# The last 1024 columns of an output projection by seven half-size products, with the weights' sums kept in DRAM

## The chip, the cores and the metric

The kernel runs on one core of a Trainium2 chip. The metric is the device time of one execution in microseconds (us), the median of several. The engines of the core are named as in the profile: PE (TensorE, the matmuls), DVE (VectorE), ACT (ScalarE), POOL (GpSimd) and SP (SyncE, which here only issues DMAs). ACT and POOL issue DMAs too. Matmul results go to PSUM banks of 128 partitions by 512 float32; everything else lies in SBUF or, for what is put aside, in DRAM.

## The reference

One layer of an encoder on 512 tokens with 2048 model columns, in float32. Eight stick-breaking heads and eight latent heads read the normed input; their gated outputs form `mixed`, 512 x 2048, and the last step is a projection, a norm and a residual:

```python
h = rms_norm(x, pre_norm_w)
p = h @ w_in                                    # all projections of the heads
o_a = stick_breaking_attention(q, k, v)         # 8 heads x 128
o_b = chunk_causal_softmax_attention(q_mla, k_mla, v_mla)   # 8 latent heads x 128
mixed = concat([o_a * silu(sb_gate), o_b * silu(mla_gate)], axis=-1)
y = mixed @ w_out                               # 512 x 2048 by 2048 x 2048
return x + rms_norm(y, post_norm_w)
```

## The kernel before

Each float32 operand of a product is held as a high and a low part (both float32r). `split` makes them: ACT casts the high part (line 96), DVE subtracts it from the value for the low part (line 99). A product of two such operands is three matmuls into the same bank, high by high, high by low and low by high (`mm3`, line 127).

TensorE runs its matmuls in the order in which they are traced. The loads on SP (`load`, line 88) keep their traced order too. A scheduler orders the rest: ACT, DVE and POOL each run their instructions one after another in an order that was fixed when the kernel was built, and each instruction waits there for its inputs and for its buffer.

The program has these stages. The latents `cq` and `ckv` are made first, to about 108 us. Then come the latent heads, to about 310 us. One iteration of their loop (line 685) is about 20 to 26 us; the filler between attention steps is the gate columns (`gps`). In an iteration POOL issues the loads of the next small weights (`mraw`, line 114), clears a part of the transposed rows `th` and `tl` (lines 588 and 589), and stores the gated head to DRAM (`put_aside`, line 607). Then come the stick-breaking heads, whose filler is the other projections and the first steps of the output projection.

The output projection `y = mixed @ w_out` has four groups of 512 columns. `out_group` makes groups 0 to 2. Each has eight weight pieces of 512 KB (two chunks of 128 rows each): SP loads a piece into the ring `raw` of N_RAW = 2 buffers, ACT casts `whi` from it, DVE subtracts `wlo`, and both of these have rings of three buffers. A chunk is multiplied with the four blocks of 128 tokens of `mixed`, whose parts (`mxh`, `mxl`, one pair for each chunk, in `msplit`) were loaded back from DRAM by POOL (line 392). One group is 16 chunks x 4 blocks x 3 = 192 matmuls of 512 columns. Group 0 ends at about 717 us, group 1 at about 760.5 and group 2 at about 804. During group 2 `resident_weights` splits ten of the last group's sixteen chunks (`woh`, `wol`).

The last group goes block by block, so that each block's norm and residual run beside the next block's products: 48 matmuls a block, and for the last block 2 x 48 of 256 columns. For each block SP loads four pieces of x (`xr`), PE makes the bank, ACT squares it (line 408) for the norm, DVE multiplies it by the norm's weight (line 410), POOL makes the factor `r` (lines 791 and 792), DVE makes the four residual pieces (line 801), and their DMAs go out alternately on SP and ACT (line 802). On SP's queue the `xr` loads of a block stand behind the two `out` DMAs of the block before it.

Of the kernel before, what the change touches and what calls it, by code (L numbers as in the profile page):

```python
# [19 lines left out]
P = 128  # L20
S = 512
# [36 lines left out]
def block(ctx: ExitStack, tc: tile.TileContext, a: dict):  # L58
# [61 lines left out]
    # TensorE runs what is traced, in that order: the order below keeps it fed.  # L120
# [131 lines left out]
    def turns(n, unit, name):  # L252
        """fraction of a turn in n * unit radians, n a whole number of at most 12 bits"""
# [34 lines left out]
    # [block, half, 32]: cosines twice; sines with the sign of their half; the queries' ones scaled  # L288
# [23 lines left out]
    def latent(banks, n, width, name):  # L312
        """The scaled projection, token-major, and the sums of squares of its first n columns."""
# [23 lines left out]
    done = {}  # L337

    def gate(t, name):
        """silu of a tile of gate columns, transposed."""  # L340
# [35 lines left out]
    # chunks of the output projection: the latent heads' first  # L376
# [24 lines left out]
    ypw = [[] for _ in range(NB)]  # L401
    y_tags = iter(["q4"] * 4 + ["row"] * 6 + ["gt"] * 2 + ["tr"] * 5)

    def out_piece(b, ps, pw):
        n = len(ypw[b])
        w = ps.shape[1]
        junk = zbank("junk")
        act.activation(out=junk[:, :w], in_=ps, func=AF.Square, scale=1.0 / math.sqrt(D), accum_out=ssy[b][:, n:n + 1])
        y = g(f"y{b}", tag=next(y_tags))[:, :w]
        dve.tensor_tensor(out=y, in0=ps, in1=pw, op=ALU.mult)  # L410
        ypw[b].append(y)

    def post_weight(gi):
        pw = g("pw", tag="tr")
        load(out=pw, in_=a["post_w"][0:1, gi * S:(gi + 1) * S].broadcast_to([P, S]))
        return pw

    w_tags = iter(["t"] * 4 + ["mv"] * 4 + ["g"] * 22)
    ws = []

    def resident_weights():
        """The next two chunks of the last columns' weights."""
        raw = ring.tile([P, 1024], F32, tag="raw", name="raw", bufs=N_RAW)
        load(out=raw, in_=a["w_o"][3, len(ws) // 2])
        for j in range(2):
            hi, lo = g("woh", F32R, next(w_tags)), g("wol", F32R, next(w_tags))
            split(hi, lo, raw[:, j * S:(j + 1) * S])
            ws.append((hi, lo))

    def out_group(gi):  # L430
        banks = [bank(f"y{b}") for b in range(NB)]
        for i in range(8):
# [4 lines left out]
            if gi == 2 and i >= 3:  # L437
                resident_weights()
            for j in range(2):
                s_ = slice(j * S, (j + 1) * S)  # L440
                split_mixed()
                for b in range(NB):
                    out_mm(banks[b], b, i * 2 + j, wh[:, s_], wl[:, s_])
                    yield
        pw = post_weight(gi)
        for b in range(NB):
            out_piece(b, banks[b], pw)

    def filler():
# [10 lines left out]
        for gi in range(3):  # L460
            yield from out_group(gi)

# [14 lines left out]
    def rotary_queries(grp, new_bank):  # L477
# [11 lines left out]
        # the two blocks of a bank are one accumulation, which the first of its products starts  # L489
# [24 lines left out]
    def rotary_turn(stacks):  # L514
        """[high; low] of four heads' rotary queries, transposed."""
# [27 lines left out]
    # rstd of every token along the free axis, on every partition  # L543
# [27 lines left out]
    def row_tiles(name):  # L571
        """The rows of the four blocks of queries, the short ones beside each other."""
# [3 lines left out]
    class Weighted:  # L576
        """(sum over s of vals[s, :]^T rows[q, s]) * gate, transposed, by blocks of keys."""
# [46 lines left out]
    class Latent:  # L624
        """Scores and softmax of a latent head."""
# [59 lines left out]
    for h in range(H + 1):  # L685
# [47 lines left out]
    for h in range(H):  # L733
# [4 lines left out]
        for b in range(NB):  # L738
# [11 lines left out]
            fill((1, 3, 3, 7)[b])  # L750
        cur = Weighted(rows, need("v", h // 4), (h % 4) * P)
# [7 lines left out]
        else:  # L759
            put_aside(h, out)  # L760

# [1 line left out]
    for _ in steps:  # L763
        pass
    pw = post_weight(3)
    for i in range(5, 8):
        wh, wl = weights(a["w_o"][3, i], 1024)
        ws += [(wh[:, :S], wl[:, :S]), (wh[:, S:], wl[:, S:])]
    for b in range(NB):
        xs = []  # L770
        for i in range(2):
            if b % 2:
                xr = [g("xr"), g("xr")]
            else:
                xr = ring.tile([P, 1024], F32, tag="raw", name="xr", bufs=N_RAW)
                xr = [xr[:, :S], xr[:, S:]]
            for j in range(2):
                load(out=xr[j], in_=a["x"][b * P:(b + 1) * P, (2 * i + j) * S:(2 * i + j + 1) * S])
            xs += xr
        cuts = [slice(0, S)] if b < NB - 1 else [slice(0, 256), slice(256, S)]  # L780
        part = tn("part")
        for n, s_ in enumerate(cuts):
            ps = bank(f"y{b}")[:, :s_.stop - s_.start]
            for c in range(16):
                out_mm(ps, b, c, ws[c][0][:, s_], ws[c][1][:, s_])
            if n == len(cuts) - 1:
                dve.tensor_reduce(out=part, in_=ssy[b][:, :3 + n], axis=AX.X, op=ALU.add)
                dve.tensor_scalar(out=part, in0=part, scalar1=EPS, scalar2=None, op0=ALU.add)
            out_piece(b, ps, pw[:, s_])
        r2 = tn("r2")  # L790
        pool.tensor_tensor(out=r2, in0=ssy[b][:, 2 + len(cuts):3 + len(cuts)], in1=part, op=ALU.add)
        pool.tensor_tensor(out=r2, in0=r2, in1=mhalf[:, :1], op=ALU.pow)
        at = 0
        for i, y in enumerate(ypw[b]):
            w = y.shape[1]
            o = xs[at // S][:, at % S:at % S + w]
            if b == NB - 1 and i == 2:
                act.activation(out=y, in_=y, func=AF.Copy, scale=r2)
                pool.tensor_tensor(out=o, in0=y, in1=o, op=ALU.add)
            else:  # L800
                dve.scalar_tensor_tensor(out=o, in0=y, scalar=r2, in1=o, op0=ALU.mult, op1=ALU.add)
            (nc.sync, nc.scalar)[i % 2].dma_start(out=a["out"][b * P:(b + 1) * P, at:at + w], in_=o)
            at += w
# [54 lines left out]
```

## Time and profile before

| what | value |
|---|---|
| time, median of 3 runs | 858.51 us (858.46 to 859.05) |
| span of the profiled execution | 857.2 us |
| PE busy | 844.1 us (98%), 4146 matmuls |
| DVE busy | 425.0 us (50%) |
| ACT busy | 337.8 us (39%) |
| POOL busy | 42.1 us (5%) |
| mean granted TensorE clock | 0.997 |
| DMA | 97.19 MB, mean 113 GB/s |

The span is the time from the first to the last instruction of one profiled execution; the median time is 1.3 us longer. A matmul's own duration in the trace overlaps that of the next, so the distance between the starts of two matmuls is what one of them costs. An engine's idle time is listed with what ended it, the releaser. The names of tiles are those of the code; "128x512 f32" is partitions by elements. Rows of DMA issues on SP and ACT (SPq, ACTq) show when the DMA was issued, not when it landed.

### The profile page before, as it was taken

How to read it: one execution, taken by the hardware profiler on the slowest of the kernel's cores; microseconds unless marked ns; L12 is line 12 of the kernel's file. 1: busy time of each engine (PE TensorE's matmuls, PEld its weight loads, DVE VectorE, ACT ScalarE, POOL GpSimd, SP SyncE). 2: the span in 40 equal slices, each digit the busy share in tenths (PEclk: the TensorE clock that was granted, in tenths of full speed). 3: DMA queues.
4: the chain of work that ended last, by engine and by line, in shares of the span. 5: the costliest groups of instructions: out<-in, count | busy, mean ns of one | idle time of the engine just before them, and what ended most of it. 6: DMA issues, size and time to landing. Idle time of an engine off the chain costs nothing.

```text
span 857.2 us, 10780 instructions
## 1 busy us (share of the span) xinstructions
PE 844.1 (98%) x4146; PEld 711.9 (83%) x4146; DVE 425.0 (50%) x757; ACT 337.8 (39%) x585; POOL 42.1 (5%) x100
## 2 busy tenths in 40 slices
PE   8999999999999999999999999999999999999995
PEld 5889988888888888888888888888888888888885
DVE  5576755556556433536354524446364623244333
ACT  6743655554454423424243314323243423134201
POOL 1010000000000110000000000000001000000001
PEclk9999999999999999999999999999999999999998
DMA  9823222222221252222222224222223232336364
GB/s 314 317 75 101 99 86 75 81 93 80 93 81 62 76 192 97 79 100 85 97 88 86 89 96 135 99 86 95 89 81 132 97 110 99 111 103 204 112 190 153
DMA packets 32627, 97.19 MB, mean 113 GB/s; under 512 B 4144, under 2 KB 4672, under 8 KB 32576
## 3 DMA queue, kind: packets, MB, share of 16 engines
q1 hardware_dynamic: 27792, 82.46, 28.5%
q0 software_dynamic: 3488, 12.08, 4.3%
q10 hardware_dynamic: 1296, 1.97, 0.7%
q8 instruction: 32, 0.52, 0.3%
q14 instruction: 19, 0.16, 0.1%
HBM read 88.37 MB, written 8.13 MB: 113 GB/s over the span
## 4 chain that ended last, share of the span: by engine, by line
PE 93%; DVE 3%; ACT 1%; DMA 1%; issue 0%; POOL 0%; DVEq 0%; SPq 0%; ACTq 0%; POOLq 0%
PE y L122 20%; PE gps L122 19%; PE qp L122 10%; PE v L122 10%; PE kp L122 10%; PE cq L122 4%; PE av L122 4%; PE mz L122 3%; PE mqp L122 3%; PE ckv L122 2%; PE tp L125 2%; PE z L122 2%; PE qrp L122 1%; PE mv L122 1%; PE mkp L122 1%; DMA raw<-in_w_cq 1%
## 5 line engine op out<-in xcount | busy, mean ns | idle before, releaser
L99 DVE TENSOR_TENSOR wlo<-raw,whi 128x1024 fp32r<-128x1024 f32 (+2 forms) x124 | 147.5, 1190 | 187.8 <-ACT whi L96 186.0
L96 ACT CAST whi<-raw 128x1024 fp32r<-128x1024 f32 (+2 forms) x124 | 127.0, 1024 | 251.5 <-PE y L122 58.4
L122 PE MATMUL gps<-hh,whi 128*128 128x512 f32 x256 | 102.0, 398 | 0.0
L122 PE MATMUL gps<-hl,whi 128*128 128x512 f32 x256 | 100.1, 391 | 0.0
L122 PE MATMUL gps<-hh,wlo 128*128 128x512 f32 x256 | 99.9, 390 | 0.0
L122 PE MATMUL y<-whi,mxh 128*128 128x512 f32 (+1 forms) x222 | 85.5, 385 | 0.0
L122 PE MATMUL y<-whi,mxl 128*128 128x512 f32 (+1 forms) x222 | 85.1, 383 | 0.0
L122 PE MATMUL y<-wlo,mxh 128*128 128x512 f32 (+1 forms) x222 | 85.1, 383 | 0.0
L122 PEld LDWEIGHTS gps<-hh,wlo 128*128 128x128 f32 x256 | 48.1, 188 | 10.6
L122 PEld LDWEIGHTS gps<-hl,whi 128*128 128x128 f32 x256 | 48.2, 188 | 7.6
L122 PEld LDWEIGHTS gps<-hh,whi 128*128 128x128 f32 x256 | 48.2, 188 | 7.5
L122 PE MATMUL qp<-hh,whi 128*128 128x512 f32 x128 | 52.0, 407 | 0.0
L96 ACT CAST th<-tp 128x512 fp32r<-128x512 f32 (+1 forms) x64 | 27.1, 423 | 63.2 <-PE tp L125 63.2
L99 DVE TENSOR_TENSOR tl<-tp,th 128x512 fp32r<-128x512 f32 (+1 forms) x64 | 31.2, 488 | 39.9 <-ACT th L96 39.5
L122 PE MATMUL v<-whi,hh 128*128 128x512 f32 x128 | 50.9, 397 | 0.0
L122 PE MATMUL qp<-hh,wlo 128*128 128x512 f32 x128 | 50.1, 391 | 0.0
L122 PE MATMUL qp<-hl,whi 128*128 128x512 f32 x128 | 50.0, 391 | 0.0
L122 PE MATMUL v<-whi,hl 128*128 128x512 f32 x128 | 49.9, 390 | 0.0
L122 PE MATMUL v<-wlo,hh 128*128 128x512 f32 x128 | 49.9, 390 | 0.0
L122 PE MATMUL kp<-hh,whi 128*128 128x512 f32 x128 | 49.8, 389 | 0.0
L122 PE MATMUL kp<-hl,whi 128*128 128x512 f32 x128 | 49.8, 389 | 0.0
L122 PE MATMUL kp<-hh,wlo 128*128 128x512 f32 x128 | 49.8, 389 | 0.0
(246 smaller groups left out, 1618.5 us busy)
## 6 DMA issues: line engine op xcount, KB each, us to landing
raw<-in_w_t SPq DMA_DIRECT2D x64, 512.0 KB, 3.2
raw<-in_w_o SPq DMA_DIRECT2D x32, 512.0 KB, 3.2
raw<-in_w_v SPq DMA_DIRECT2D x16, 512.0 KB, 3.2
xs<-in_x SPq DMA_DIRECT2D x16, 256.0 KB, 6.2
xr<-in_x SPq DMA_DIRECT2D x16, 256.0 KB, 4.9
xt<-in_xt SPq DMA_DIRECT2D x15, 256.0 KB, 5.7
mixed<-mix POOLq DMA_DIRECT2D x15, 256.0 KB, 2.3
mx<-mixed POOLq DMA_DIRECT2D x15, 256.0 KB, 3.4
```

The source lines that it names most:

```text
L96: i = act.copy(out=hi, in_=src)
L99: dve.tensor_tensor(out=lo, in0=src, in1=hi.bitcast(F32), op=ALU.subtract)
L122: tc.keep_in_program_order(pe.matmul(out=out, lhsT=lhsT, rhs=rhs, start=start, stop=stop, **kw))
L125: tc.keep_in_program_order(pe.transpose(out, in_, identity))
```

## The change

Groups 0 and 1 stay. Groups 2 and 3 are now one product of 512 tokens x 2048 by 2048 x 1024, cut in halves: tokens A1 and A2 of 256, K of 1024, columns of 512. The Strassen-Winograd scheme makes the four quarters of the result from seven products instead of eight. Each product is 8 chunks x 2 blocks x 3 = 48 matmuls of 512 columns (`product`), and the last one is made block by block, its second block in halves of 256 columns. The order is x = A11 w11, z = S1 (w_sums 0), y = S2 (w_sums 2), v = S3 (w_sums 1) and into the same banks A22 (w_sums 3), then A12 w21 into the banks of x, then S4 w22. S1 to S4 are sums of quarters of `mixed`; w_sums 0 to 3 are sums of quarters of the weights.

`weight_sums(j)` makes the weights' sums: four loads of 256 KB by POOL, four DVE subtractions 128x512, four stores of 256 KB to DRAM by POOL. It is called eight times, 32 of each in all (16.8 MB moved). They are traced among the stick-breaking heads; the order that is built puts them among the latent heads. `first_sums` and `last_sum` load chunks of `mixed` again and make and split S1, S2, S4 (groups 0 and 1) and S3, which takes the place of a part of `msplit`. The last head's chunk is now put in DRAM too. The ring `raw` has four buffers in place of two. The `xr` tiles come from other slots. The results of the block pair 2, 3 are complete first, so their residuals come first.

```diff
-SLOTS = {"g": 46, "q4": 4, "row": 6, "tr": 4, "t": 4, "gt": 2, "mv": 4, "qrt": 8}
-N_RAW = 2
+SLOTS = {"g": 48, "q4": 4, "row": 6, "tr": 4, "t": 4, "gt": 2, "mv": 4, "qrt": 8}
+N_RAW = 4
...
+    def sum_piece(b, at, ps, u, pw, junk):
+        w = ps.shape[1]
+        y = g(f"y{b}", tag=next(y_tags))[:, :w]
+        dve.tensor_tensor(out=y, in0=ps, in1=u, op=ALU.add)
+        square_sum(b, y, junk[:, :w])
+        dve.tensor_tensor(out=y, in0=y, in1=pw, op=ALU.mult)
+        ypw[b][at] = y
...
-            if gi == 2 and i >= 3:
-                resident_weights()
+            if 4 <= 8 * gi + i < 12:
+                first_sums(8 * gi + i - 4)
...
+            if gi == 1 and i >= 4:
+                last_sum(2 * i - 8)
+                last_sum(2 * i - 7)
...
+    def weight_sums(j):
+        i, c = j // 2, slice((j % 2) * S, (j % 2 + 1) * S)
+        b11, b12, b22, b21 = (g("wsum", tag="qrt") for _ in range(4))
+        for t, gi, k in ((b11, 2, 0), (b12, 3, 0), (b22, 3, 4), (b21, 2, 4)):
+            pool.dma_start(out=t, in_=a["w_o"][gi, k + i][:, c])
+        for n, (out, x, y) in enumerate(((b11, b12, b11), (b12, b22, b12), (b22, b22, b11), (b21, b21, b22))):
+            dve.tensor_tensor(out=out, in0=x, in1=y, op=ALU.subtract)
+            pool.dma_start(out=w_sums[n][i][:, c], in_=out)
...
+    def product(banks, which, srcs, start, stop):
+        for i in range(4):
+            wh, wl = weights(srcs[i], 1024)
+            for j in (2 * i, 2 * i + 1):
+                s_ = slice((j % 2) * S, (j % 2 + 1) * S)
+                for r in range(2):
+                    mm3(banks[r], *factor(which, j, r), wh[:, s_], wl[:, s_], start and j == 0, stop and j == 7,
+                        skip_group_check=True)
+                    yield
...
+        v = [bank("sv") for _ in range(2)]
+        yield from product(v, "S3", w_sums[1], True, False)
+        for r in range(2):
+            sum_piece(2 + r, 3 * S, v[r], s15[r], pw3, junk)
+        yield from product(v, "A22", w_sums[3], False, True)
+        for r in range(2):
+            sum_piece(2 + r, 2 * S, v[r], s1[r], pw2, junk)
+        kept = []
+        for i in range(4):
+            raw = ring.tile([P, 1024], F32, tag="raw", name="raw", bufs=N_RAW)
+            load(out=raw, in_=w22[i])
+            for j in range(2):
+                hi, lo = g("woh", F32R, ("g", "qrt")[j]), g("wol", F32R, ("g", "qrt")[j])
+                split(hi, lo, raw[:, j * S:(j + 1) * S])
+                kept.append((hi, lo))
+        yield from product(x, "A12", w21, False, True)
+        for r in range(2):
+            out_piece(r, 2 * S, x[r], pw2, junk)
+        for b in (2, 3):
+            residual(b)
+        for b in (0, 1):
+            cuts = [slice(0, S)] if b == 0 else [slice(0, 256), slice(256, S)]
+            for s_ in cuts:
+                ps = zbank("sp")[:, :s_.stop - s_.start]
+                for j in range(8):
+                    mm3(ps, *factor("S4", j, b), kept[j][0][:, s_], kept[j][1][:, s_], j == 0, j == 7)
+                    yield
+                sum_piece(b, 3 * S + s_.start, ps, s15[b][:, s_], pw3[:, s_], junk)
+            residual(b, b == 1)
...
-        for gi in range(3):
+        for gi in range(2):
             yield from out_group(gi)
+        yield from last_columns()
...
+        if h < H - 1:
+            weight_sums(h)
+        if h == H // 2:
+            weight_sums(H - 1)
...
-            put_aside(h, out)
+        put_aside(h, out)
...
-    nc = bacc.Bacc("TRN2", target_bir_lowering=False, num_devices=1)
+    nc = bacc.Bacc("TRN2", target_bir_lowering=False, num_devices=1, dynamic_dma_scratch_size=4096)
```

Three places of the order in which the engines run it. The first is POOL among the latent heads, from the store of head 1 to the clearing of `th` and `tl` in iteration h = 3 (172 to 190 us of the trace of before). Before, POOL issues:

```order
L607 DMA mixed_1223<-mix 128x512
L114 DMA mraw<-in_w_head 128x768
L114 DMA mraw<-in_w_kvv 128x512
L588 MEMSET th 128x128
L589 MEMSET tl 128x128
```

In the changed kernel the store of that head is `mixed_1227`; from the second load of small weights on, the loads of weights (`wsum`) and the stores of sums (`w_sums_592` to `w_sums_595` are w_sums 0 to 3) stand between:

```order
L114 DMA mraw<-in_w_head 128x768
L466 DMA wsum<-in_w_o 128x512
L469 DMA w_sums_592<-wsum 128x512
L469 DMA w_sums_593<-wsum 128x512
L114 DMA mraw<-in_w_kvv 128x512
L466 DMA wsum<-in_w_o 128x512
L469 DMA w_sums_594<-wsum 128x512
L466 DMA wsum<-in_w_o 128x512
L469 DMA w_sums_595<-wsum 128x512
L466 DMA wsum<-in_w_o 128x512
L730 MEMSET th 128x128
L731 MEMSET tl 128x128
```

So the load of `mraw` and the two clearings now stand behind stores that wait for DVE, and loads that wait for a free buffer.

The second is DVE in the same iteration (184 to 192 us of before): `tl`, `mlo` and `mkl` are low parts that PE reads next, `mz` are scores in PSUM and `ri`, `p` belong to the softmax. Before:

```order
L99 TENSOR_TENSOR tl<-tp,th 128x512
L99 TENSOR_TENSOR mlo<-mraw,mhi 128x768
L99 TENSOR_TENSOR mkl<-mkp,mkh 128x512
L99 TENSOR_TENSOR tl<-tp,th 128x384
L658 MEMSET mz 64x64
L660 TENSOR_REDUCE nm<-mz 128x1
L658 MEMSET mz 64x64
L663 RECIPROCAL ri<-sm 128x1
```

After, four subtractions of the weights' sums (`wsum`) stand among them:

```order
L99 TENSOR_TENSOR tl<-tp,th 128x512
L468 TENSOR_TENSOR wsum<-wsum 128x512
L99 TENSOR_TENSOR mlo<-mraw,mhi 128x768
L99 TENSOR_TENSOR mkl<-mkp,mkh 128x512
L468 TENSOR_TENSOR wsum<-wsum 128x512
L99 TENSOR_TENSOR tl<-tp,th 128x384
L800 MEMSET mz 64x64
L802 TENSOR_REDUCE nm<-mz 128x1
L800 MEMSET mz 64x64
L468 TENSOR_TENSOR wsum<-wsum 128x512
L805 RECIPROCAL ri<-sm 128x1
```

Each of them waits there for a load, and what stands below it waits with it.

The third is the end of the program, DVE first. Before, the first block's residual follows its product's multiplication by the norm's weight:

```order
L99 TENSOR_TENSOR wlo<-raw,whi 128x1024
L410 TENSOR_TENSOR y_6965<-y_6912,pw 128x512
L801 SCALAR_TENSOR_TENSOR xr<-y_6297,r_6967,xr 128x512
L801 SCALAR_TENSOR_TENSOR xr<-y_6559,r_6967,xr 128x512
L801 SCALAR_TENSOR_TENSOR xr<-y_6871,r_6967,xr 128x512
L801 SCALAR_TENSOR_TENSOR xr<-y_6965,r_6967,xr 128x512
```

After, these rows begin at the end of the A22 product (`sv` are its banks) and lead to the first residual, that of block 2; the four `wlo` are those of the A12 product:

```order
L423 TENSOR_TENSOR y_7267<-sv,s_6948 128x512
L99 TENSOR_TENSOR wlo<-raw,whi 128x1024
L423 TENSOR_TENSOR y_7271<-sv,s_6949 128x512
L425 TENSOR_TENSOR y_7267<-y_7267,pw 128x512
L99 TENSOR_TENSOR wlo<-raw,whi 128x1024
L425 TENSOR_TENSOR y_7271<-y_7271,pw 128x512
L99 TENSOR_TENSOR wlo<-raw,whi 128x1024 x2
L587 SCALAR_TENSOR_TENSOR xr<-y_6502,r_7404,xr 128x512
L587 SCALAR_TENSOR_TENSOR xr<-y_6868,r_7404,xr 128x512
L587 SCALAR_TENSOR_TENSOR xr<-y_7267,r_7404,xr 128x512
```

The first residual now stands behind all weights of the A12 product. On SP's queue the end of before reads:

```order
L88 DMA raw<-in_w_o 128x1024 x13
L88 DMA pw<-in_post_w 128x512 x2
L88 DMA raw<-in_w_o 128x1024 x3
L88 DMA xr<-in_x 128x512 x4
L802 DMA out<-xr 128x512 x2
L88 DMA xr<-in_x 128x512 x4
```

and after:

```order
L88 DMA raw<-w_sums_593 128x1024 x4
L88 DMA raw<-w_sums_595 128x1024 x4
L88 DMA raw<-in_w_o 128x1024 x8
L88 DMA xr<-in_x 128x512 x4
L588 DMA out<-xr 128x512 x2
L88 DMA xr<-in_x 128x512 x4
```

The alternation of `xr` and `out` for the four blocks is as before, now for blocks 2, 3, 0, 1.

## Rows read from the trace of the kernel before

**Rows 1.** The page: busy time and share of the span, then the chain by engine.

```profile
PE 844.1 (98%) x4146; PEld 711.9 (83%) x4146; DVE 425.0 (50%) x757; ACT 337.8 (39%) x585; POOL 42.1 (5%) x100
...
PE 93%; DVE 3%; ACT 1%; DMA 1%; issue 0%; POOL 0%; DVEq 0%; SPq 0%; ACTq 0%; POOLq 0%
```

**Rows 2.** The chain that ended last, from 640 us: start, length, what.

```profile
683.75 164.55 PE y L122 x771
...
849.78 0.75 DVE xr L801
...
851.20 1.80 DVE xr L801 x2
```

**Rows 3.** Timeline of PE: group 2's end, and the last block's halves.

```profile
803.30 0.39 PE L122 MATMUL y<-whi,mxh 128*128 128x512 f32 x1
...
803.98 0.39 PE L122 MATMUL y<-woh,mxh 128*128 128x512 f32 x1
...
837.33 0.28 PE L122 MATMUL y<-woh,mxh 128*128 128x256 f32 x1
...
837.69 0.28 PE L122 MATMUL y<-woh,mxh 128*128 128x256 f32 x1
```

**Rows 4.** Groups by line and shape, 717 to 858 us: busy, mean ns.

```profile
L99 DVE TENSOR_TENSOR wlo<-raw,whi 128x1024 fp32r<-128x1024 f32 x17 | 20.8, 1225 | 49.7 <-ACT whi L96 49.7
L96 ACT CAST whi<-raw 128x1024 fp32r<-128x1024 f32 x17 | 17.9, 1052 | 49.8 <-PE y L122 37.2 <-DMA raw<-in_w_o 12.6
...
L410 DVE TENSOR_TENSOR y<-y,pw 128x512 f32<-128x512 f32 x14 | 9.6, 692 | 26.4 <-ACT junk L408 26.3
```

**Rows 5.** DMA issues of the page: KB each, median us to landing.

```profile
raw<-in_w_o SPq DMA_DIRECT2D x32, 512.0 KB, 3.2
...
mx<-mixed POOLq DMA_DIRECT2D x15, 256.0 KB, 3.4
```

**Rows 6.** Timeline of DVE at the end: the residuals of blocks 2 and 3.

```profile
838.48 2.74 DVE L801 SCALAR_TENSOR_TENSOR xr<-y,r,xr 128x512 f32<-128x512 f32 x4 [0.19 <-POOL r L792]
...
849.78 3.21 DVE L801 SCALAR_TENSOR_TENSOR xr<-y,r,xr 128x512 f32<-128x512 f32 x4 [0.47 <-POOL r L792]
```

**Rows 7.** Timeline of SP's queue at the end.

```profile
839.26 1.67 SPq L802 DMA_DIRECT2D out<-xr  x2
841.04 2.08 SPq L88 DMA_DIRECT2D xr<-in_x  x4
850.56 2.84 SPq L802 DMA_DIRECT2D out<-xr  x3
```

**Rows 8.** The tile xr, 800 to 858 us.

```profile
DMA to landing us min/median/max: 2.5/3.9/5.9
```

**Rows 9.** Busy time by engine in the latent heads, 151 to 247 us.

```profile
151.00:247.00 96.00, 96.00 (x501) 82.02 (x501) 57.21 (x127) 49.86 (x94) 7.85 (x19) 1.00 0.25 85
```

**Rows 10.** Timeline of POOL, 150 to 250 us.

```profile
180.32 0.55 POOL L114 DMA_DIRECT2D mraw<-in_w_head  x1 [7.01 <-DVE mlo L99]
186.42 0.55 POOL L114 DMA_DIRECT2D mraw<-in_w_kvv  x1 [5.55 <-DVE mlo L99]
189.83 0.20 POOL L588 MEMSET th<- 128x128 f32 x1 [2.87 <-PE av L122]
```

**Rows 11.** Timeline of DVE in two iterations of the latent heads.

```profile
187.45 0.56 DVE L99 TENSOR_TENSOR tl<-tp,th 128x384 fp32r<-128x384 f32 x1 [0.72 <-ACT th L96]
...
191.21 0.16 DVE L663 RECIPROCAL ri<-sm 128x1 f32<-128x1 f32 x1 [1.59 <-ACT p L662]
...
224.81 0.95 DVE L99 TENSOR_TENSOR mlo<-mraw,mhi 128x768 fp32r<-128x768 f32 x1
```

**Rows 12.** Timeline of PE there: who reads these two low parts.

```profile
189.43 0.34 PE L122 MATMUL av<-tl,mv 128*128 128x384 f32 x1
...
225.82 0.50 PE L122 MATMUL mqp<-cqth,mlo 128*128 128x512 f32 x1
```

**Rows 13.** Waits of PE over the whole span: total, times, longest.

```profile
PE cq L122 <- DVE wlo L99: 1.0, 2, 0.8
...
PE cq L122 <- ACT whi L96: 0.4, 1, 0.4
```

More of the change, by code (lines that the diff above doesn't have):

```diff
@@ L400, in block, with square_sum, out_piece, post_weight @@
     ssy = [const.tile([P, 5], F32, name=f"ssy{b}") for b in range(NB)]
[L401 to L405, printed above, removed]
+    ypw = [{} for _ in range(NB)]
+    y_tags = iter(["q4"] * 4 + ["row"] * 6 + ["gt"] * 2 + ["tr"] * 4 + ["g"])
+    def square_sum(b, ps, junk):
+        n = pieces[b]
+        pieces[b] += 1
+        act.activation(out=junk, in_=ps, func=AF.Square, scale=1.0 / math.sqrt(D), accum_out=ssy[b][:, n:n + 1])
+    pieces = [0] * NB
+    def out_piece(b, at, ps, pw, junk=None):
         w = ps.shape[1]
-        junk = zbank("junk")
-        act.activation(out=junk[:, :w], in_=ps, func=AF.Square, scale=1.0 / math.sqrt(D), accum_out=ssy[b][:, n:n + 1])
+        square_sum(b, ps, (zbank("junk") if junk is None else junk)[:, :w])
         y = g(f"y{b}", tag=next(y_tags))[:, :w]
         dve.tensor_tensor(out=y, in0=ps, in1=pw, op=ALU.mult)
-        ypw[b].append(y)
-    def post_weight(gi):
-        pw = g("pw", tag="tr")
+        ypw[b][at] = y
[5 more added lines that the diff above has]
+        dve.tensor_tensor(out=y, in0=y, in1=pw, op=ALU.mult)
+        ypw[b][at] = y
+    def post_weight(gi, tag="tr"):
+        pw = g("pw", tag=tag)
         load(out=pw, in_=a["post_w"][0:1, gi * S:(gi + 1) * S].broadcast_to([P, S]))
         return pw
[L418 to L428, printed above, removed]
     def out_group(gi):
@@ L444, in out_group @@
                     yield
+            if gi == 1 and i >= 4:
+                last_sum(2 * i - 8)
+                last_sum(2 * i - 7)
         pw = post_weight(gi)
         for b in range(NB):
-            out_piece(b, banks[b], pw)
+            out_piece(b, gi * S, banks[b], pw)
+    HALF = S // 2
+    sums = {}
+    w_sums = [dram.tile([4, P, 1024], F32, name=f"w_sums{n}") for n in range(4)]
+    def weight_sums(j):
[6 more added lines that the diff above has]
+            pool.dma_start(out=w_sums[n][i][:, c], in_=out)
@@ new lines, in mixed_again, with first_sums @@
+    def mixed_again(n):
+        t = g("mx", tag="mv")
+        pool.dma_start(out=t, in_=mixed[order[n]])
+        return t
+    def first_sums(j):
+        x, y = mixed_again(j), mixed_again(j + 8)
+        t, s4 = g("st", tag="tr"), g("st4", tag="tr")[:, :HALF]
+        s1, s2 = t[:, :HALF], t[:, HALF:]
+        dve.tensor_tensor(out=s1, in0=x[:, HALF:], in1=y[:, HALF:], op=ALU.add)
+        dve.tensor_tensor(out=s2, in0=s1, in1=x[:, :HALF], op=ALU.subtract)
+        dve.tensor_tensor(out=s4, in0=y[:, :HALF], in1=s2, op=ALU.subtract)
+        h12, l12, hl4 = g("s12h", F32R), g("s12l", F32R), g("s4", F32R)
+        split(h12, l12, t)
+        split(hl4[:, :HALF], hl4[:, HALF:], s4)
+        sums[j] = h12, l12, hl4
@@ new lines, in last_sum, with factor @@
+    def last_sum(j):
+        x = mixed_again(j)
+        s3 = x[:, HALF:]
+        dve.tensor_tensor(out=s3, in0=x[:, :HALF], in1=s3, op=ALU.subtract)
+        split(msplit[j][0][:, HALF:], msplit[j][1][:, HALF:], s3)
+    def factor(which, j, r):
+        lo_, hi_ = slice(r * P, (r + 1) * P), slice(HALF + r * P, HALF + (r + 1) * P)
+        if which in ("S1", "S2"):
+            c = lo_ if which == "S1" else hi_
+            return sums[j][0][:, c], sums[j][1][:, c]
+        if which == "S4":
+            return sums[j][2][:, lo_], sums[j][2][:, hi_]
+        k, c = {"A11": (0, lo_), "S3": (0, hi_), "A12": (8, lo_), "A22": (8, hi_)}[which]
+        return msplit[j + k][0][:, c], msplit[j + k][1][:, c]
@@ new lines, in residual @@
+    def residual(b, tail=False):
+        xs = []
+        for i in range(4):
+            xr = g("xr")
+            load(out=xr, in_=a["x"][b * P:(b + 1) * P, i * S:(i + 1) * S])
+            xs.append(xr)
+        n = pieces[b]
+        part = tn("part")
+        dve.tensor_reduce(out=part, in_=ssy[b][:, :n - 1], axis=AX.X, op=ALU.add)
+        dve.tensor_scalar(out=part, in0=part, scalar1=EPS, scalar2=None, op0=ALU.add)
+        r2 = tn("r2")
+        pool.tensor_tensor(out=r2, in0=ssy[b][:, n - 1:n], in1=part, op=ALU.add)
+        pool.tensor_tensor(out=r2, in0=r2, in1=mhalf[:, :1], op=ALU.pow)
+        for i, (at, y) in enumerate(sorted(ypw[b].items())):
+            w = y.shape[1]
+            o = xs[at // S][:, at % S:at % S + w]
+            if tail and i == 2:
+                act.activation(out=y, in_=y, func=AF.Copy, scale=r2)
+                pool.tensor_tensor(out=o, in0=y, in1=o, op=ALU.add)
+            else:
+                dve.scalar_tensor_tensor(out=o, in0=y, scalar=r2, in1=o, op0=ALU.mult, op1=ALU.add)
+            (nc.sync, nc.scalar)[i % 2].dma_start(out=a["out"][b * P:(b + 1) * P, at:at + w], in_=o)
@@ L758, in block @@
             last_mixed[0] = out
-        else:
-            put_aside(h, out)
+        put_aside(h, out)
     for _ in steps:
         pass
[L765 to L803, printed above, removed]
 def _layout(x, positions, pre_norm_w, w_in, q_norm_w, w_q_up, kv_norm_w, w_kv_up, w_out, post_norm_w):
```

19 lines of the change are left out of this document (added).

## The prediction

> **What bounds the kernel now.** I read the page first: PE is busy for 98% of the span, and 93% of the chain that ended last is PE [rows 1]. In the chain the reader is to see one stretch, 164.55 us of output projection from 683.75 us on without a break, and behind it 8.9 us of norm, residual and stores (848.3 to 857.2), of which DVE's residual is the visible part [rows 2]. So time is won where matmuls are taken away, if nothing else then ends later. The span of this execution is 857.2 us, 1.3 us less than the median of 858.51; I make the sum on the span and add 1.3 at the end.
>
> **What is removed.** The distance between starts is the price of a matmul: three of 512 columns take 803.98 - 803.30 = 0.68 us, 0.227 each; three of 256 columns take 837.69 - 837.33 = 0.36, 0.12 each [rows 3]. Before, the last 1024 columns are 192 + 144 matmuls of 512 columns and 96 of 256. After, they are six products of 48 plus 24 (312 of 512 columns) and 48 of 256. The difference is 24 x 0.227 + 48 x 0.12 = 5.4 + 5.8 = 11.2 us of PE time. If PE stays the bound with the same 8.9 us behind it, the span is 846.0.
>
> **The middle, which I cost at almost nothing.** Six DVE sums of the products' results, reloads of `mixed` and their splits lie in groups 0 and 1 and among products of 10.9 us each. A product's weights need four casts of 1.05 us and four subtractions of 1.23 us [rows 4], so ACT and DVE are under half busy, and the weights have four buffers in place of two with loads that land in 3.2 us [rows 5]. That cover goes only where DVE or ACT is queued behind something late. The one exception is that A22 accumulates in banks that DVE must read first: about one DVE addition of 0.69 us [rows 4] less the 0.3 us by which the first bank is ready before the second, 0.4 us. Let T be the start of the A22 product. Four products after group 1 is the time at which group 2 ends now, 803.98 [rows 3], so T = 804.0 + 0.4 = 804.4. By PE alone, A22 ends at T + 10.9, A12 at T + 21.7, S4 at T + 32.9.
>
> **The tail, which gives half of it back.** The first residual (block 2) stands in DVE's order behind the last `wlo` of the A12 product. From the end of A22 at T + 10.9 DVE has two additions, two multiplications (0.69 each) and four `wlo` (1.23 each) [rows 4], 7.7 us, so it starts at T + 18.3 to T + 18.6; between T + 17.4 and T + 19.5 I take T + 18.3 = 822.7.
>
> From there a loop through SP's queue begins. Each block's `xr` loads stand behind the second `out` of the block before, which waits for that block's third residual piece. In the trace the `xr` loads are issued at 841.04, that is 2.56 us after the residual began at 838.48 [rows 6, 7]. They land 2.5 to 5.9 us later, median 3.9 [rows 8]; four are issued over 2.08 us, so I take 4.1 us to the first landing and 5.9 us to the third, both from the first issue. Then the third residual piece takes 0.65 us (a quarter of 2.74 [rows 6]) and the `out` issue another 0.6. From one block's `xr` issue to the next that is 5.9 + 0.65 + 0.6 = 7.15 us, and 7.8 for block 3, where a multiplication of 0.69 stands between. So block 1's loads are issued at 822.7 + 2.6 + 7.8 + 7.15 = 840.25, its residual begins at 844.3, and its last piece, one load later and behind the ACT and POOL step, is done about 3.4 us after that, at 847.7. In the trace the residuals end at 849.78 + 3.21 = 853.0 and the span at 857.2 [rows 6], 4.2 us of store; so the span ends at about 852.0.
>
> Today this loop is hidden: a block's products last 10.9 us and the loop needs about 7.2. In the changed kernel three turns of the loop come after T + 18.3, while PE has only 14.6 us left. If PE were the bound, it would end at 804.4 + 32.9 = 837.3. It also stalls at the start of A12: the kept weights and A12's share four `raw` buffers, and A12's first `wlo` stands behind an addition that needs A22's end, so it is ready at T + 10.9 + 0.69 + 1.23 = T + 12.8 where PE wants it at T + 11.1; 1 to 3.7 us, I take 1.7. PE then ends at 839, and 8.9 us after that gives 847.9: the loop ends later by 4 us and swallows the stall. So the tail returns about 6 of the 11.2 us.
>
> **The latent heads, which cost something.** The 32 loads, 32 subtractions and 32 stores of weights' sums run from about 151 to 247 us. PE is busy for all 96.00 us there, DVE for 57.2, POOL for 7.9 [rows 9]. DVE gains 32 x 0.69 = 22 us and POOL 64 x 0.55 = 35 us (the issue of a DMA, [rows 10]); neither is full after that, at 79 and 43 of 96 us. What matters is what waits in order. A subtraction waits for a load that costs 0.55 us to issue and 3.4 us to land (the nearest row, [rows 5]), the load waits for a buffer that a store must free, and below the subtraction stand low parts that PE reads next. Of these `tl` has a slack of 189.43 - 188.01 = 1.4 us, and the `mlo` that opens iteration h = 5 has 225.82 - 225.76 = 0.06 [rows 11, 12]. The softmax has idle time to give (1.59 us before `ri`, [rows 11]).
>
> The cost is bounded below by the work alone at the two openings without slack, 2 x (0.69 - 0.06) = 1.3 us, or nothing if the loads come early and DVE's idle time takes it; it is bounded above by a whole round trip of 4 us in each of five iterations, 20 us. Walking through the order I find three places where a load is issued less than a round trip before its subtraction: the opening of h = 3, and iterations 4 and 5, at about 1 us each, an estimate from these rows. I take 3 us, near the lower end, since most subtractions stand where DVE waits today. The four weight buffers may give back part of the 1.4 us that PE waits for `whi` and `wlo` in the first product [rows 13]; I take 0.5.
>
> POOL issued its DMAs in 0.55 us while DVE was 60% busy [rows 9, 10]. The Trainium skill, page "SBUF — State Buffer", section "SBUF: two separate sides", speaks against a change like this one: a DMA issued from POOL can stand still while DVE runs an instruction that holds the shared ports, about 3100 ns against 620 alone. By that page's longer figure 64 x 3.1 = 198 us, an estimate from it, would not fit in 96 us; the rows of before agree with the shorter one.
>
> **The sum.** 852.0 + 3 - 0.5 = 854.5, plus 1.3: 855.8, say 856.0 us; 11.2 off PE, some 6 back in the tail, 3 in the latent heads.
>
> **Rivals.** (1) *PE stays the bound.* If `xr` lands nearer to the 2.5 us end and the subtractions hide, the span is 847.9 + 0 to 1.5 and the time 849 to 851. For it: PE is the bound today. Against it: the order on SP. (2) *The subtractions stall PE.* DVE stands at subtractions whose loads are late, because POOL's queue is itself held up by stores that wait for DVE; `th` and `tl` are cleared late, `mraw` is loaded late. At 2.6 us (a round trip of 4.0 less a slack of 1.4) in each of five iterations that is 13 us: 852.0 + 13 + 1.3 = 866, slower than before. It decides from 7 us of stalls on (852.0 + 7 + 1.3 = 860.3). For it: slack of 0.06 at two places and a queue in which both engines wait for each other. Against it: a third of DVE's time there is idle. (3) *The loop is longer.* If the first `xr` also lands at 5 us and the third at 7, each cycle is 1.1 longer, 3.3 in all: 859, no change. (4) *POOL's issues stand still behind DVE.* If each of the 64 new issues waits out one long DVE instruction (1.23 us for a `wlo` [rows 4]) it takes 0.55 + 1.23 = 1.8 us, 114 in all; with the 7.9 of today POOL is full for 122 us of a stretch of 96, and the latent heads grow by 26: 852.0 + 26 + 1.3 = 879. Against it: issues of 0.55 us beside a DVE that is 60% busy. That is the mechanism of the rule of "SBUF — State Buffer" above.
>
> **How the numbers follow.** A difference of 0.2% (1.7 us) is about what a measurement of this kernel can tell from no change: under 856.8 is faster, over 860.2 slower. The forecast has 0.47, and its own range is 853 to 859.5: an early start of the loop (T + 17.4) and no cost in the latent heads give 852.5, a late start and 5 us there 859. Rival 1 has 0.15, rival 2 has 0.22, rival 3 has 0.13, rival 4 has 0.03. Faster: 0.30 of the forecast, 0.15 of rival 1 and 0.03 of rival 3, 0.48. Slower: rivals 2 and 4 with 0.25 and 0.03 of the others' ends, 0.28. Same: the rest, 0.24. The range leaves out about one in ten on either side: 849.5, inside rival 1, to 865.0, the middle of rival 2.
>
> **What would show it.** The profile after should have 48 x 6 + 24 matmuls of 512 columns for the last 1024 columns, and PE's work 11 us shorter. The step on the tail is right if PE ends about 13 us before the span (8.9 today) and each block's residual begins when its first `xr` lands, about 7 us apart. It is wrong if the residuals of blocks 0 and 1 follow their products. The step on the latent heads is right if PE waits some 3 us in all between 150 and 250 us, for `mlo`, `mhi` or `tl`; the waits of DVE for `wsum` loads tell how near rival 2 came. The prediction is wrong most easily there, since no row of before shows a subtraction that waits for a load from POOL.

## The result: 24 us longer, in two places ahead of the tail

The changed kernel takes 883.05 us (882.44 to 883.35, 4 runs) where the kernel before takes 858.78 in the same comparison: a ratio of 1.0274, 95% interval 1.0257 to 1.0291. The profiled execution has a span of 881.3 us against 857.2. The forecast was 856.0 us with a range of 849.5 to 865.0, so the time lies outside the range and on the other side of no change.

The page of the changed kernel, to be laid beside [rows 1]: busy time, then the chain by engine.

```profile
PE 844.3 (96%) x4074; PEld 706.7 (80%) x4074; DVE 485.3 (55%) x869; ACT 360.4 (41%) x622; POOL 91.2 (10%) x189
...
PE 77%; DMA 10%; issue 5%; DVE 4%; ACT 2%; POOL 1%; SPq 1%; DVEq 0%; POOLq 0%; ACTq 0%
```

The chain that was 93% PE is now 77% PE and 10% DMA: loads have come onto the path. (PE's busy time did not fall, though 72 matmul records are fewer. One reason is that part of the matmuls ran at half clock, below.)

To find where the time went I use marks, matmuls that both traces have. The first and the last row of the latent queries `mqp`, and the first of the output projection `y` and of A11's product `sx`, from the views of these tiles (count, shortest/median/longest ns, first and last start). Before, then after:

```profile
L122 PE MATMUL mqp<-cqth,mhi x32: 389/389/474, 107.0 to 273.3; 128*128 128x512 f32 x32
...
L122 PE MATMUL y<-whi,mxh x222: 283/389/481, 669.8 to 847.8; 128*128 128x512 f32 x105, 128*128 128x256 f32 x6
```

```profile
L122 PE MATMUL mqp<-cqth,mhi x32: 389/389/628, 107.5 to 290.3; 128*128 128x512 f32 x32
...
L122 PE MATMUL y<-whi,mxh x128: 389/389/792, 686.8 to 787.8; 128*128 128x512 f32 x128
...
L122 PE MATMUL sx<-whi,mxh x32: 388/389/495, 788.4 to 855.5; 128*128 128x512 f32 x32
```

Before, group 2 begins 192 matmuls of 0.2265 us ahead of 803.98, at 760.5. So, stage by stage:

| stretch | before | after | difference |
|---|---|---|---|
| start to the first `mqp` | 107.0 | 107.5 | +0.5 |
| latent heads, first to last `mqp` | 166.3 | 182.8 | +16.5 |
| to the first `y` | 396.5 | 396.5 | 0 |
| groups 0 and 1 | 90.7 | 101.6 | +10.9 |
| the last 1024 columns to the end | 96.7 | 92.9 | -3.8 |
| span | 857.2 | 881.3 | +24.1 |

PE's waits in the changed kernel, over the whole span, name the two places; [rows 13] has none of these:

```profile
PE y L122 <- DVE y L416: 8.7, 1, 8.7
PE mv L122 <- DVE mv L99: 3.0, 2, 2.8
PE mz L122 <- DVE mkl L99: 2.9, 1, 2.9
PE mqp L122 <- DVE mlo L99: 2.0, 1, 2.0
...
```

**The latent heads.** The stretch of [rows 9] after the change (PE, PEld, DVE, ACT, POOL busy, granted clock, DMA share):

```profile
151.00:247.00 96.00, 86.93 (x419) 71.42 (x418) 60.82 (x127) 42.11 (x78) 32.40 (x63) 0.95 0.60 203
```

PE stands for 9.1 us, and the clock granted to it is 0.95. DVE is no fuller than before (60.8 against 57.2): it waits. The whole stretch from the first `mqp` to the last, before and then after, shows what the loss is made of:

```profile
107.00:273.70 166.70, 166.01 (x865) 141.69 (x863) 99.64 (x217) 87.72 (x161) 11.45 (x29) 1.00 0.24 81
```

```profile
107.00:290.70 183.70, 173.78 (x868) 145.21 (x867) 117.45 (x249) 87.57 (x161) 46.70 (x93) 0.97 0.48 164
```

PE stands for 9.9 us where it stood for 0.7, and it is busy for 7.8 us longer for the same work, in part at half clock. One place where it stands, DVE's timeline first, then POOL's, then PE's:

```profile
211.18 0.69 DVE L99 TENSOR_TENSOR tl<-tp,th 128x512 fp32r<-128x512 f32 x1
215.43 0.69 DVE L468 TENSOR_TENSOR wsum<-wsum 128x512 f32<-128x512 f32 x1 [3.57 <-DMA wsum<-in_w_o]
216.04 0.69 DVE L99 TENSOR_TENSOR mlo<-mraw,mhi 128x512 fp32r<-128x512 f32 x1
216.64 0.69 DVE L99 TENSOR_TENSOR mkl<-mkp,mkh 128x512 fp32r<-128x512 f32 x1
```

```profile
209.15 0.55 POOL L466 DMA_DIRECT2D wsum<-in_w_o  x1
...
213.69 0.55 POOL L466 DMA_DIRECT2D wsum<-in_w_o  x1 [2.61 <-DMA w_sums<-wsum]
216.42 0.54 POOL L469 DMA_DIRECT2D w_sums<-wsum  x1 [2.18 <-DVE wsum L468]
```

```profile
217.38 0.39 PE L122 MATMUL mz<-mkl,mqh 128*128 128x256 f32 x1 [2.90 <-DVE mkl L99]
```

The subtraction at 215.43 waits for the load issued at 209.15, which took 6.3 us to land, the slowest of the 32 (median 3.6). `mlo` and `mkl` stand behind it in DVE's queue, their own inputs long there, and PE waits 2.90 us for `mkl`. POOL stands meanwhile: it waits 2.61 us for a store to land and free a buffer, and 2.18 us for DVE before its next store. An earlier place shows a load that is late because it was issued late. POOL waits for a subtraction, then DVE for the load (which landed in 3.5 us), and PE waits 2.05 us for the `mlo` that stands behind:

```profile
177.26 0.55 POOL L466 DMA_DIRECT2D wsum<-in_w_o  x1 [0.79 <-DVE wsum L468]
```

```profile
180.83 0.69 DVE L468 TENSOR_TENSOR wsum<-wsum 128x512 f32<-128x512 f32 x1 [2.57 <-DMA wsum<-in_w_o]
```

Each queue holds the other.

**Groups 0 and 1.** DVE's and PE's timelines at the border of the two groups (L481 is the first addition of a sum of `mixed`, L493 the S3 subtraction, L416 the multiplications that free group 0's banks):

```profile
725.50 0.43 DVE L481 TENSOR_TENSOR st<-mx 128x256 f32<-128x256 f32 x1 [4.44 <-DMA mx<-mixed]
...
733.48 0.43 DVE L481 TENSOR_TENSOR st<-mx 128x256 f32<-128x256 f32 x1 [2.31 <-DMA mx<-mixed]
...
739.83 0.43 DVE L493 TENSOR_TENSOR mx<-mx 128x256 f32<-128x256 f32 x1 [2.17 <-DMA mx<-mixed]
...
741.64 2.48 DVE L416 TENSOR_TENSOR y<-y,pw 128x512 f32<-128x512 f32 x4
```

```profile
733.26 0.39 PE L122 MATMUL y<-whi,mxl 128*128 128x512 f32 x1
742.38 0.79 PE L122 MATMUL y<-whi,mxh 128*128 128x512 f32 x1 [8.73 <-DVE y L416]
742.97 0.63 PE L122 MATMUL y<-wlo,mxh 128*128 128x512 f32 x1
743.40 0.63 PE L122 MATMUL y<-whi,mxl 128*128 128x512 f32 x1
```

It is the same pattern as in the second place above. Group 0's results are in the banks at 733.7; the four multiplications that would free them stand behind the last of the eight sums and behind four of the S3 subtractions. Two of these wait for a reload of `mixed` (2.31 and 2.17 us), and POOL issues the second of these reloads only when a sum on DVE has freed its buffer:

```profile
736.01 1.22 POOL L473 DMA_DIRECT2D mx<-mixed  x2 [4.84 <-DVE st L482]
```

PE waits 8.73 us and then runs at half clock (0.43 us from start to start instead of 0.227) for about twelve matmuls, which makes the 8.7 into 10.9.

**The tail.** DVE's and SP's timelines at the end, to be laid beside [rows 6, 7]:

```profile
850.80 2.74 DVE L587 SCALAR_TENSOR_TENSOR xr<-y,r,xr 128x512 f32<-128x512 f32 x4
...
858.21 0.75 DVE L587 SCALAR_TENSOR_TENSOR xr<-y,r,xr 128x512 f32<-128x512 f32 x1 [4.41 <-DMA xr<-in_x]
...
873.81 0.75 DVE L587 SCALAR_TENSOR_TENSOR xr<-y,r,xr 128x512 f32<-128x512 f32 x1 [2.04 <-DMA xr<-in_x]
```

```profile
853.35 2.10 SPq L88 DMA_DIRECT2D xr<-in_x  x4
858.99 2.86 SPq L588 DMA_DIRECT2D out<-xr  x2
861.95 1.92 SPq L88 DMA_DIRECT2D xr<-in_x  x4
867.20 2.17 SPq L588 DMA_DIRECT2D out<-xr  x2
869.46 1.95 SPq L88 DMA_DIRECT2D xr<-in_x  x4
```

The residuals wait for `xr`, and the `xr` loads go out 8.6 and 7.5 us apart, each behind the `out` of the block before. PE's last matmul ends at 867.5; the span ends 13.8 us later, where it was 8.9.

### The profile page after: what moved, and what is told of

It is laid out like the page before. It is cut to its first block, busy times and chain, and to the rows that moved or that the text cites. A ratio compares the mean times of both kernels' runs of the same rounds, so it can differ in the third digit from the quotient of the medians.

```text
span 881.3 us, 11034 instructions
## 1 busy us (share of the span) xinstructions
PE 844.3 (96%) x4074; PEld 706.7 (80%) x4074; DVE 485.3 (55%) x869; ACT 360.4 (41%) x622; POOL 91.2 (10%) x189
## 4 chain that ended last, share of the span: by engine, by line
PE 77%; DMA 10%; issue 5%; DVE 4%; ACT 2%; POOL 1%; SPq 1%; DVEq 0%; POOLq 0%; ACTq 0%
PE gps L122 16%; PE qp L122 10%; PE v L122 10%; PE kp L122 10%; PE y L122 6%; PE cq L122 4%; DMA wsum<-in_w_o 4%; PE av L122 3%; DMA xr<-in_x 2%; PE ckv L122 2%; PE sv L122 2%; DMA mx<-mixed 2%; PE mz L122 2%; PE z L122 2%; PE tp L125 2%
## 5 line engine op out<-in xcount | busy, mean ns | idle before, releaser
L99 DVE TENSOR_TENSOR wlo<-raw,whi 128x1024 fp32r<-128x1024 f32 (+2 forms) x137 | 163.3, 1192 | 144.1 <-ACT whi L96 141.3
L96 ACT CAST whi<-raw 128x1024 fp32r<-128x1024 f32 (+2 forms) x137 | 140.5, 1026 | 215.3 <-PE kp L122 42.6
L122 PE MATMUL y<-whi,mxh 128*128 128x512 f32 x128 | 51.3, 401 | 8.7 <-DVE y L416 8.7
L122 PEld LDWEIGHTS gps<-hl,whi 128*128 128x128 f32 x256 | 48.8, 191 | 7.8
L122 PE MATMUL y<-wlo,mxh 128*128 128x512 f32 x128 | 50.8, 397 | 0.0
L122 PE MATMUL y<-whi,mxl 128*128 128x512 f32 x128 | 50.7, 396 | 0.0
```

Source lines behind the costliest of these rows:

```text
L96: i = act.copy(out=hi, in_=src)
L99: dve.tensor_tensor(out=lo, in0=src, in1=hi.bitcast(F32), op=ALU.subtract)
L122: tc.keep_in_program_order(pe.matmul(out=out, lhsT=lhsT, rhs=rhs, start=start, stop=stop, **kw))
```

## The experiments

Experiments 1 to 7 are one execution each. Four executions of the changed kernel lie within 0.9 us and those of the kernel before within 2.5, so a difference of 1 to 2 us between single executions tells little. Experiments 1, 2, 5 and 6 ran on one chip, the others on another; the kernel before took 858.92 us on the first and 858.75 on the second.

**1. No weights' sums.**

```diff
-        if h < H - 1:
-            weight_sums(h)
-        if h == H // 2:
-            weight_sums(H - 1)
...
-        yield from product(z, "S1", w_sums[0], True, True)
+        yield from product(z, "S1", w11, True, True)
```

(and `w22`, `w21`, `w22` for the other three).

> The changed kernel without its weights' sums: the 32 loads, 32 subtractions and 32 stores are left out, and the four products that read them read pieces of w_out of the same size instead, so the result is not the layer's. In the changed kernel the last matmul row of the latent heads comes 16.4 us later than before, relative to the first one. Theory (the sums' subtractions hold DVE's queue up among the latent heads): that stretch is as long as before within 1 us, and the span falls from 881.3 to 864 to 866. Rival (something else among the latent heads, such as four weight buffers or another order of DVE): the stretch stays more than 8 us longer than before and the span over 872.

Measured: span 864.3, 866.07 us; `mqp` from 107.1 to 273.5, 166.4 us. The sums make all of the 16.5 us; four weight buffers and the rest of the order cost nothing there.

**2. No subtractions.** Loads and stores stay.

```diff
-            dve.tensor_tensor(out=out, in0=x, in1=y, op=ALU.subtract)
             pool.dma_start(out=w_sums[n][i][:, c], in_=out)
```

> The changed kernel without the 32 subtractions alone: the loaded pieces are stored as they are, so the sums are wrong. Theory (DVE's queue stands at a subtraction whose load is late, and the low parts behind it are late): the latent heads lose at most 4 us of the 16.4, the span is 865 to 869. Rival (POOL's queue, full of loads and stores that wait, brings the small weights and the clearings late, or the traffic slows other loads): 10 us or more stay, the span is 875 or more.

Measured: span 882.6, 884.35 us; `mqp` from 110.0 to 292.7, 182.7 us (2.5 us of the span lie in the late start). My theory in its plain form fell: without one subtraction on DVE the latent heads lose the same 16.4 us. PE's and POOL's waits show another way to the same loss, the rival's: PE's waits over the span, POOL's for 120 to 330 us, and ACT's cast of a small weight.

```profile
PE mz L122 <- ACT mkh L96: 9.6, 1, 9.6
...
PE av L122 <- POOL th L729: 2.3, 1, 2.3
```

```profile
POOL w_sums L468 <- DMA wsum<-in_w_o: 40.3, 26, 3.3
POOL wsum L466 <- DMA w_sums<-wsum: 26.0, 16, 3.2
```

```profile
202.09 0.83 ACT L96 CAST mhi<-mraw 128x768 fp32r<-128x768 f32 x1 [12.74 <-DMA mraw<-in_w_head]
```

POOL's queue stands at stores that wait for loads and at loads that wait for stores, and the load of a small weight stands in it too: ACT waits 12.74 us for it. With the subtractions gone the order on POOL is another one as well, so this shows that POOL's queue can cost as much, not that it did in the changed kernel, where no cast of a small weight (`mhi`) waits for a load. The next two kernels separate the queues.

**3. What the latent heads need from POOL is taken off it.**

```diff
-        pool.dma_start(out=raw[:, :n], in_=src)
+        act.dma_start(out=raw[:, :n], in_=src)
...
-                pool.memset(tokens(th, 2).bitcast(F32), 0.0)
-                pool.memset(tokens(tl, 2).bitcast(F32), 0.0)
+                dve.memset(tokens(th, 2).bitcast(F32), 0.0)
+                dve.memset(tokens(tl, 2).bitcast(F32), 0.0)
```

> The changed kernel with what the latent heads need from POOL taken off it: the loads of the small weights are issued by ACT, and th and tl are cleared by DVE. Nothing is left out. The weights' sums still use POOL for loads and stores and DVE for subtractions. Theory (DVE's queue standing at late subtractions is a path of its own): most of the 16.4 us in the latent heads stays, 10 us or more, the span is 874 or more. Rival (the loss comes by way of POOL's queue, which brings the small weights late): under 5 us stay, the span is under 870.

Measured: span 883.7, 885.39 us; `mqp` from 107.2 to 293.4, 186.2 us:

```profile
L122 PE MATMUL mqp<-cqth,mhi x32: 389/390/474, 107.2 to 293.4; 128*128 128x512 f32 x32
```

With what the latent heads need taken off POOL's queue, 19.9 us are lost. That is more than in the changed kernel, and not all of it need be DVE's alone: ACT, which now issues the small loads, stands twice until DVE has freed the buffer (`mlo`), from ACT's waits between 107 and 295 us:

```profile
ACT th L96 <- DVE mlo L99: 3.4, 2, 2.5
```

**4. The same, and no subtractions.**

> The same without the 32 subtractions (the loaded pieces are stored as they are, so the sums are wrong). Without the subtractions alone the latent heads lost as much as with them, and PE waited for small weights that POOL loads. Theory (the two queues are two paths, and either of them is enough): with both taken away the latent heads are within 2 us of before, the span is 863 to 868. Rival (the DMA traffic of the sums slows the latent heads by itself): 5 us or more stay, the span is 870 or more.

Measured: span 862.7, 864.45 us; `mqp` from 107.1 to 273.4, 166.3 us, as before the change:

```profile
L122 PE MATMUL mqp<-cqth,mhi x32: 389/389/474, 107.1 to 273.4; 128*128 128x512 f32 x32
```

The traffic was all there (DMA share and GB/s are the last two columns, after the granted clock):

```profile
200.00:250.00 50.00, 50.00 (x262) 42.67 (x262) 31.33 (x70) 27.72 (x50) 18.49 (x34) 1.00 0.75 255
```

So DMA engines that are 75% busy cost PE nothing in this stretch, and neither do the loads that ACT now issues. There are two paths, DVE's queue (19.9 us in experiment 3, with ACT's waits in it) and POOL's (16.4 in experiment 2); with neither the loss is gone. In the changed kernel PE's waits name DVE's results, so there it came by way of DVE's queue, whose loads POOL issued late.

**5. The subtractions later.** The same work, kept behind what was traced before it, so among the stick-breaking heads.

```diff
-            dve.tensor_tensor(out=out, in0=x, in1=y, op=ALU.subtract)
+            tc.keep_in_program_order(dve.tensor_tensor(out=out, in0=x, in1=y, op=ALU.subtract))
```

> The changed kernel with each subtraction of the weights' sums kept behind the DVE instruction that was traced before it, so that all 32 run among the stick-breaking heads, their first eight loads long before. Nothing is left out. Theory (it is the place in DVE's queue, a round trip behind the load, that costs): the latent heads are as long as before within 1 us, the stick-breaking heads grow by 0 to 4 us, the span is 865 to 870. Rival (the work itself, 22 us of DVE and 35 us of POOL, costs wherever it stands): the span stays over 875.

Measured: span 866.6, 868.38 us; `mqp` from 107.5 to 273.7, 166.2 us. From there to the first `y` (671.5) are 397.8 us, 1.3 more than before, which is no more than single executions differ by. The work is nearly free; its place in the two queues cost 16.5.

**6. The sums of `mixed` in traced order**, the first addition and the S3 subtraction alike:

```diff
-        dve.tensor_tensor(out=s1, in0=x[:, HALF:], in1=y[:, HALF:], op=ALU.add)
+        tc.keep_in_program_order(dve.tensor_tensor(out=s1, in0=x[:, HALF:], in1=y[:, HALF:], op=ALU.add))
```

> The changed kernel with the first addition of each sum of mixed, and each S3 subtraction, kept behind the DVE instruction traced before it. DVE's order then has group 0's four multiplications, which free PE's banks, after six of these sums in place of eight and two S3 subtractions. In the changed kernel PE waits 8.7 us there and runs at half clock for a while after. Theory (the multiplications stand in DVE's queue behind sums whose reloads of mixed are late): the wait falls to 0 to 3 us, groups 0 and 1 together from 101.8 to 91 to 95 us, the span to 872 to 875. Rival (the banks are free late for another reason, the squares on ACT or PE's own weights): the wait stays over 6 us.

Measured: span 869.3, 871.36 us. Groups 0 and 1 take 90.3 us (686.7 to 777.0), the wait for L416 is gone, and so is the half clock there. DVE's timeline, now with the multiplications ahead of the last two sums:

```profile
730.37 0.42 DVE L481 TENSOR_TENSOR st<-mx 128x256 f32<-128x256 f32 x1
...
732.55 2.49 DVE L416 TENSOR_TENSOR y<-y,pw 128x512 f32<-128x512 f32 x4
...
736.74 0.42 DVE L481 TENSOR_TENSOR st<-mx 128x256 f32<-128x256 f32 x1
```

The gain was larger than I expected of it, and the span is below the 872 to 875 of the expectation: no wait is left, where I had allowed up to 3 us. (In the changed kernel four S3 subtractions stood ahead of the multiplications, not two.)

**7. The residuals' loads ahead of the stores.**

```diff
+        for b in (2, 3, 0, 1):
+            xload(b)
         for b in (2, 3):
             residual(b)
```

(`xload` is the loop of four `xr` loads taken out of `residual`.)

> The changed kernel with all sixteen loads of x for the residuals traced, and so queued on SP, ahead of the first residual's stores. Nothing is left out. In the changed kernel PE ends at 867.4 us and the span 13.9 us later. Theory (the loop xr load, residual, out, next xr load through SP's queue sets the end): blocks 2 and 3 are done before PE ends, block 1's residual follows its last product as before the change, and the span ends 9 to 10 us after PE, 876 to 878. Rival (the stores or the residuals' own work set the end, or PE's end is late too): the span ends over 12 us after PE.

Measured: span 873.0, 875.01 us. PE's last matmul ends at 863.2 and the span 9.8 us later; SP's queue has the sixteen loads in one piece:

```profile
839.97 14.26 SPq L88 DMA_DIRECT2D xr<-in_x  x16
854.32 15.15 SPq L595 DMA_DIRECT2D out<-xr  x9
```

So the loop through SP cost 13.8 - 9.8 = 4.0 us. The other 4.3 of the 8.3 us lie ahead of the edit: the latent heads took 180.3 us and groups 0 and 1 99.6, in the same order of instructions as in the changed kernel.

**8. The three moves (5, 6, 7) together.**

> Three changes of order together: the subtractions of the weights' sums among the stick-breaking heads, the sums of mixed kept in traced order, the residuals' loads ahead of the stores. Nothing is left out. If the three losses are separate, 14.7 + 12.0 us as the first two measured alone and about 4 in the tail come off 881.3: a span of 850 to 852 and a time of 851 to 854, faster than before by 0.5 to 0.9%. If they hide one another, the time is 855 to 860, the same as before.

Measured: 853.21 us (852.78 to 854.61) against 858.75, a ratio of 0.993, interval 0.9914 to 0.9947, 0.7% faster than the kernel before, and far under the 883.05 of the changed kernel. The span of the profiled execution is 852.8, 0.8 over what I expected; it is the slowest of the four, and the others have spans of 851.0 to 851.5. In it the first `mqp` comes at 109.3, 1.8 us later than in the changed kernel. PE waits 1.3 us for a first piece of weights there, and then the granted clock is 0.50 for 3.4 us, in which PE starts ten matmuls where the changed kernel starts sixteen (at clock 1.00):

```profile
14.80:18.20 3.40, 3.40 (x10) 2.62 (x9) 2.08 (x3) 3.12 (x9) 0.00 (x0) 0.50 1.05 413
```

Why that load came late is open. The three losses were separate: 14.7 + 12.0 + 4.0 from 881.3 gives 850.6, and 1.8 of the 2.2 us between lie in that start.

## Why the prediction was wrong, step by step

- **What is removed** was right: the products of the last columns run at the distances of [rows 3], and from 788.4 to the last matmul PE needs 79.1 us where it needed 87.8; the 11.2 us less 2.2 of stalls are there within 0.3.
- **The tail** was right. A22 started at 832.51, the first residual at 850.80, 18.3 us later as forecast; the first `xr` loads went out 2.55 us after it (2.56). The cycles were 8.6 and 7.5 us for 7.8 and 7.15, and the end came at T + 48.8 for T + 47.6. The A22 stall was 0.38 (0.4), that at A12 1.6 (1.7). Experiment 7 shows the loop and its price.
- **The latent heads** are the step that failed most: I took 3 us, and it was 16.5. Rival 2 had the mechanism ("a queue in which both engines wait for each other") and a price of 13; I gave it 0.22. What was wrong is how the estimate was made. I asked at which places a load was issued less than a round trip before its subtraction, with POOL's issues taken as on time, found three, and gave each 1 us. But a subtraction that is late makes the next store late, that the next load, and that the next subtraction: the round trips add up in a loop, and DVE waited 21.4 us at twelve of the 32 subtractions. The loads were slower too: the twelve that DVE waited for landed 3.2 to 6.3 us after their issue, where I took 3.4 for all. With 3.4 each, and issued when they were, DVE would have waited some 13 us, an estimate from these twelve. The argument against rival 2, that a third of DVE's time is idle, left out the added work: by my own sum DVE is busy for 79 of 96 us with it. My upper bound of one round trip in each of five iterations, 20 us, was nearer to the result, but by luck: PE stood for 9.2 us more than before, and the rest of the loss is PE being busy for longer after the waits, in part at half clock, a term that no part of the prediction has.
- **The middle, "almost nothing",** was wrong by 10.9 us, and no rival had it. The step looked at whether DVE and ACT are busy enough to be late (under half), and not at the order: it said that the cover goes "where DVE or ACT is queued behind something late", and did not go on to the reloads of `mixed`, of which four buffers allow two sums at a time, or to what stands behind them, the multiplications that free PE's banks.
- **The four weight buffers** gave nothing back that can be seen: +0.5 us at the start where I took -0.5, and in experiment 1, which has the four buffers too, the first `mqp` comes at 107.1 (107.0 before). PE's waits for `whi` and `wlo` did fall, from 1.4 to 1.0 us, but PE's first product `cq` began 0.5 us later (5.6 for 5.1).
- **Rival 4**, POOL's issues standing still behind DVE, did not come. The 32 loads of weights were issued in 546 to 553 ns each, and the 32 stores in 539 to 767, beside a DVE that was 63% busy. The Trainium skill, page "SBUF — State Buffer", section "SBUF: two separate sides", gives about 3100 ns for a DMA of this kind that overlaps with a DVE `tensor_copy`; the subtractions here are of another kind, `TENSOR_TENSOR`, and no run here shows such a time. What POOL lost it lost in waits.

With the terms as measured the sum closes: 852.0 + 16.5 + 10.9 + 0.5 + 1.2 (the longer tail) = 881.1, for 881.3.

## What to carry to other kernels

An engine that is half idle is no cover for work that waits. Before costing an added instruction at nothing, look at what it waits for at its place in the queue, what stands behind it, and whether what it waits for waits in turn on the same queue: then round trips add up, and it is these that have to be counted, not the work alone. The same 22 us of DVE and 35 of POOL cost 16.5 us where each subtraction stood close behind its load, and about 1.3 where DVE found the loads landed.

## What the runs showed of the hardware

- After a stall PE can run at half clock (1.2 GHz in place of 2.4), and not always. The kernels of the result and of experiment 7 have the same order of instructions up to the tail, and in both PE stands for 2.05 us before the same matmul. In the first the granted clock then is 0.50 from 184.4 to 187.7 us, and PE starts 11 matmuls in these 3.30 us; in the second it stays at 1.00, and PE starts 18. PE's row and the stretch behind it, granted clock third from the end, for the first and then the second:

```profile
183.38 0.50 PE L122 MATMUL mqp<-cqth,mlo 128*128 128x512 f32 x1 [2.05 <-DVE mlo L99]
```

```profile
184.40:187.70 3.30, 3.30 (x11) 2.56 (x10) 1.35 (x3) 0.45 (x1) 1.05 (x2) 0.50 0.88 288
```

```profile
183.20 0.50 PE L122 MATMUL mqp<-cqth,mlo 128*128 128x512 f32 x1 [2.05 <-DVE mlo L99]
```

```profile
184.20:187.50 3.30, 3.30 (x18) 2.70 (x17) 2.42 (x5) 1.08 (x2) 1.06 (x2) 1.00 0.92 322
```

  The latent heads took 182.8 us in the first and 180.3 in the second, at a clock of 1.00 throughout, although PE stood there a little longer in all (11.0 us for 9.9), in more and shorter waits. What decides whether the clock falls is not shown.

- A load of 256 KB issued by POOL landed 2.2 to 6.3 us after its issue, median 3.6, while the DMA engines were 60% busy (151 to 247 us); I had taken 3.4 for all of them.
